# The first feed-forward matrix by seven block products, the second one afterwards from DRAM

## The chip, the cores and the metric

The kernel runs on one core of a Trainium2 chip. The metric is the device time of one execution in microseconds, as the median of several. The profile is that of one further execution; its span is what its trace covers.

## The reference

A trunk of two layers over 1024 tokens of width 1024. Layer 0 mixes tokens by a state-space recurrence, layer 1 by dilated attention; behind each stands the same feed-forward block, of 2816 features. Only that block and its neighbours matter here:

```python
def conv_glu_ffn(x, w_up, conv_w, conv_b, w_down):
    hcat = x @ w_up                       # 1024x1024 by 1024x5632
    hp = jnp.pad(hcat, ((0, 0), (CONV_WIDTH - 1, 0), (0, 0)))
    hcat = conv_b + sum(conv_w[k] * hp[:, CONV_WIDTH - 1 - k:CONV_WIDTH - 1 - k + seq]
                        for k in range(CONV_WIDTH))
    val, gate = jnp.split(hcat, 2, axis=-1)
    return (jax.nn.silu(gate) * val) @ w_down     # 1024x2816 by 2816x1024

h = post_norm(h, mix, ln_gain[layer, 0], ln_bias[layer, 0])
ffn = conv_glu_ffn(h, ffn_w_up[layer], ...)
h = post_norm(h, ffn, ln_gain[layer, 1], ln_bias[layer, 1])
```

post_norm is a layer norm of a weighted sum of h and the block's result. Everything is computed in float32.

## The kernel before

**Products.** A float32 product is done as three matmuls (mm3, L86 to L90): each operand x is split into hi, a rounded copy, and lo = x - hi (split, L81): ACT makes hi (L83), DVE lo (L84). The three are hi by hi, hi by lo, lo by hi. One matmul instruction takes a 128x128 block of weights and 512 columns.

**Order.** Engines run independently, each its own list of instructions in order. That list is fixed when the kernel is built, by a scheduler that follows the program's order and the free buffers of the pools. All loads and stores spoken of here are issued by SP, in SP's order, onto one queue.

**The feed-forward block** (ffn, 22 tiles of 128 features, each a value tile and a gate tile). out_proj leaves eight accumulators of 128 tokens by 1024, normalized without gain and bias; to_T (L160) turns them on PE (32 transposes for each half of the tokens), applies gain and bias and splits them into hT. For each feature tile, `up` loads 512 KB of weights, splits them (wh, wl) and does 2 halves of tokens x 8 x 3 = 48 matmuls into a PSUM tile of 1024 tokens; the causal convolution over three tokens is one ACT instruction (L208) and two DVE instructions (L212) that read PSUM; then silu on ACT (L218), the product on DVE (L219), and a split (ah, al). `down` takes two features at a time (CH = 2): for each of eight token tiles it does 2 x 6 matmuls (L236), and DVE adds the PSUM tile to the accumulator (L242 the first time, L246 after), so up and down alternate through the whole block. ln_affine (L134, L135) puts gain and bias on the eight accumulators by 16 instructions on POOL at the block's start, and `after` (ln_apply in layer 0, ln_final with L141, L145, L146 and L148 in layer 1) ends each token tile. Behind layer 0's block the values of the attention are computed from another to_T.

Pools: xp "x" 16 buffers, rawp 2 (loaded weights), wp 4 (their splits), the block's own "x" 14 and "wd" 4, PSUM "mm" 3 tiles of two banks and "tp" 2 banks.

Of the kernel before, what the change touches and what calls it, by code (L numbers as in the profile page):

```python
# [39 lines left out]
class Net:  # L40
# [119 lines left out]
    def to_T(self, accs, hf, li, xp, tmp):  # L160

        nc = self.nc
        res = []
        for k in range(KT):
            ps = self.psp.tile([P, 512], F32, "tp")
            for q in range(4):
                nc.tensor.transpose(ps[:, q * P : q * P + P], accs[4 * hf + q][:, k * P : k * P + P], self.ident[:])
            x = xp.tile([P, 2, 512], F32R, "x", "hT")
            if k % 2 == 0:
                two = tmp[0].tile([P, 2, 512], F32, tmp[1], "tmp")  # L170
# [1 line left out]
            gain, bias = (self.lnT[:, li, i, k : k + 1] for i in range(2))
            if k % 2:
                nc.vector.tensor_scalar(out=t, in0=ps[:], scalar1=gain, scalar2=bias, op0=ALU.mult, op1=ALU.add)  # L174
            else:
                nc.scalar.activation(t, ps[:], AF.Identity, bias=bias, scale=gain)
# [4 lines left out]

    def ffn(self, l, accs, hT, xp, wd_pool, first_half, after):

        nc = self.nc
# [6 lines left out]
        def start(ft, halves=(0, 1)):
            w = self.wload(a["w_up"][l, ft])
            ps = self.psp.tile([P, T], F32, "mm", "up")
            self.type1(ps, w, hT, halves)
            return w, ps

        def up(f):
            u = []
            for s in range(2):
                ft = f + s * NF  # L200
                if ft in early:
                    w, ps = early[ft]
                    self.type1(ps, w, hT, (1,))
                else:
                    w, ps = start(ft)
                t = xp.tile([P, T], F32, "x", "u")
                tf = t[:]
                nc.scalar.activation(  # L208
                    tf, ps[:], AF.Identity, bias=cw[:, 3, ft : ft + 1], scale=cw[:, 0, ft : ft + 1]
                )  # L210
# [8 lines left out]
            nc.vector.tensor_tensor(out=vf, in0=vf, in1=gf, op=ALU.mult)  # L219
            hi = xp.tile([P, T], F32R, "x", "ah")  # L220
            lo = xp.tile([P, T], F32R, "x", "al")
            self.split(vf, hi[:], lo[:])
            return hi, lo

        def load_down(c, pool, tag):
            return [self.wload(a["w_down"][l, f], pool=pool, tag=tag) for f in c]

        def down(ws, aT, first, last):
            for tt in range(8):
                ps = self.psp.tile([P, D], F32, "mm", "dn")  # L230
                sl = slice(tt * P, tt * P + P)
                for i, (w, x) in enumerate(zip(ws, aT)):
                    ah, al = x[0][:, sl], x[1][:, sl]
# [1227 lines left out]
```

## Time and profile before

| | |
|---|---|
| median of 3 runs | 3149.09 us (3148.43 to 3156.55) |
| profiled execution | 3147.12 us |
| its span | 3145.1 us |
| mean granted clock of TensorE | 0.968 of full speed |
| PE, DVE, ACT, POOL busy | 94%, 51%, 29%, 10% of the span |

The profiled execution takes 2.0 us more than its span and 2.0 us less than the median. Busy is the time in which an engine executes; a matmul's end is modelled, and matmuls overlap, so the rate at which they follow each other is read from counts in a window, not from a mean duration. In a timeline's row the two numbers are the start and the time to the end of a run of like instructions; what stands in brackets is how long the engine had been idle before, and what released it.

### The profile page before, as it was taken

Reading aid. Unit: us, or ns where it says so; the run is one execution under the profiler, and the core shown is the slowest. Engines: PE = TensorE matmul, PEld = TensorE weight load, DVE = VectorE, ACT = ScalarE, POOL = GpSimd, SP = SyncE. Lnnn points to the kernel's source line nnn. Section 1 sums busy time; section 2 is a strip of 40 time slices with the busy share of each in tenths; the row PEclk is TensorE's granted clock in tenths of the full one; section 3 lists DMA queues with packets and bytes.
Section 4 is the critical chain, followed back from the end, with each engine's and each line's share of the span. In section 5 each row is a group of like instructions: output and inputs, shape, how many; then the busy total and the mean of one; then the engine's idle time right before and its main releaser. Section 6 shows DMA issues by size and latency. Waiting matters only on the chain. (4 is left out here: it accounts for less than half of the span.)

```text
span 3145.1 us, 36960 instructions
## 1 busy us (share of the span) xinstructions
PE 2964.7 (94%) x14454; PEld 2456.0 (78%) x14454; DVE 1598.8 (51%) x2773; ACT 922.7 (29%) x1589; POOL 329.7 (10%) x247
## 2 busy tenths in 40 slices
PE   4689999999999999999999999999688999999997
PEld 3668778888888878998777777777567888888886
DVE  8964774544445561113544444344558544544447
ACT  2433332212222231113433344333424322221222
POOL 7920050000000000000000000000253200000001
PEclk8889999999999999999999999999799999999999
DMA  5242421111111143326555456555443111111112
GB/s 176 58 124 63 132 68 53 47 41 47 60 48 47 55 141 101 108 71 163 148 152 150 133 141 151 145 134 137 141 148 102 59 41 54 60 47 41 41 60 74
DMA packets 144926, 295.76 MB, mean 94 GB/s; under 512 B 19057, under 2 KB 60769, under 8 KB 144753
## 3 DMA queue, kind: packets, MB, share of 16 engines
q1 hardware_dynamic: 142640, 283.97, 31.1%
q0 software_dynamic: 2112, 9.44, 0.9%
q8 instruction: 114, 1.87, 0.3%
q14 instruction: 60, 0.48, 0.0%
HBM read 192.08 MB, written 35.20 MB: 72 GB/s over the span
## 5 line engine op out<-in xcount | busy, mean ns | idle before, releaser
L84 DVE TENSOR_TENSOR wl<-raw,wh 128x1024 fp32r<-128x1024 f32 x262 | 336.4, 1291 | 738.7 <-ACT wh L83 737.0
L83 ACT CAST wh<-raw 128x1024 fp32r<-128x1024 f32 x262 | 273.3, 1051 | 1210.5 <-PE up L89 602.3
L89 PE MATMUL up<-hT,wh 128*128 128x512 f32 x1408 | 548.6, 390 | 7.7 <-DVE hT L84 7.7
L90 PE MATMUL up<-hT,wl 128*128 128x512 f32 x1408 | 548.0, 389 | 1.9 <-DVE wl L84 1.9
L88 PE MATMUL up<-hT,wh 128*128 128x512 f32 x1408 | 547.2, 390 | 0.9 <-ACT wh L83 0.9
L88 PE MATMUL qk<-hT,wh 128*128 128x512 f32 x768 | 309.3, 403 | 10.4 <-DVE ql L433 10.4
L89 PEld LDWEIGHTS up<-hT,wh 128*128 128x128 f32 x1408 | 264.3, 188 | 65.6 <-DVE hT L84 11.0
L90 PEld LDWEIGHTS up<-hT,wl 128*128 128x128 f32 x1408 | 264.3, 188 | 57.2 <-DVE wl L84 2.8
L89 PE MATMUL qk<-hT,wh 128*128 128x512 f32 x768 | 308.9, 402 | 0.0
L88 PEld LDWEIGHTS up<-hT,wh 128*128 128x128 f32 x1408 | 264.0, 188 | 56.2 <-ACT wh L83 1.7
L90 PE MATMUL qk<-hT,wl 128*128 128x512 f32 x768 | 307.8, 401 | 0.0
L246 DVE TENSOR_TENSOR acc<-acc,dn 128x1024 f32<-128x1024 f32 x144 | 175.1, 1217 | 117.1 <-PE dn L236 114.8
L212 DVE SCALAR_TENSOR_TENSOR u<-up,cw,u 128x1022 f32<-128x1022 f32 (+1 forms) x176 | 224.6, 1278 | 10.3 <-ACT u L208 8.0
L236 PE MATMUL dn<-wh,ah 128*128 128x512 f32 x704 | 216.9, 389 | 0.0
L236 PE MATMUL dn<-wl,ah 128*128 128x512 f32 x704 | 216.7, 389 | 0.0
L236 PE MATMUL dn<-wh,al 128*128 128x512 f32 x704 | 216.6, 389 | 0.0
L84 POOL TENSOR_TENSOR gT<-oraw,gT 128x512 fp32r<-128x512 f32 x14 | 18.0, 1302 | 1796.2 <-ACT gT L83 1791.8
L88 PEld LDWEIGHTS qk<-hT,wh 128*128 128x128 f32 x768 | 148.3, 193 | 41.8 <-DVE ql L433 12.4
L89 PEld LDWEIGHTS qk<-hT,wh 128*128 128x128 f32 x768 | 148.5, 193 | 29.0
L90 PEld LDWEIGHTS qk<-hT,wl 128*128 128x128 f32 x768 | 148.0, 193 | 29.6
L88 PE MATMUL v<-wh,hT 128*128 128x512 f32 x384 | 152.8, 400 | 1.0 <-DVE tmp L174 1.0
L236 PEld LDWEIGHTS dn<-wl,ah 128*128 128x128 f32 x704 | 132.1, 188 | 27.5
(250 smaller groups left out, 4534.7 us busy)
## 6 DMA issues: line engine op xcount, KB each, us to landing
raw<-in_w_up SPq DMA_DIRECT2D x88, 512.0 KB, 3.5
qs<-qh SPq DMA_DIRECT2D x288, 128.0 KB, 2.4
raw<-in_w_out SPq DMA_DIRECT2D x48, 512.0 KB, 3.5
kl<-ql SPq DMA_DIRECT2D x192, 128.0 KB, 2.4
raw<-in_w_down SPq DMA_DIRECT2D x44, 512.0 KB, 3.5
raw<-in_w_v SPq DMA_DIRECT2D x26, 512.0 KB, 3.7
vscr<-vs SPq DMA_DIRECT2D x48, 256.0 KB, 2.3
V<-vscr SPq DMA_DIRECT2D x24, 512.0 KB, 4.4
```

The lines of the kernel that those rows point to most:

```text
L83: nc.scalar.copy(hi, x)
L84: (eng or nc.vector).tensor_tensor(out=lo, in0=x, in1=hi.bitcast(F32), op=ALU.subtract)
L88: nc.tensor.matmul(out, lh, rh, start=first, stop=False)
L89: nc.tensor.matmul(out, lh, rl, start=False, stop=False)
L90: nc.tensor.matmul(out, ll, rh, start=False, stop=last)
L212: nc.vector.scalar_tensor_tensor(out=tf[:, d:], in0=ps[:, : T - d], scalar=cw[:, d, ft : ft + 1], in1=tf[:, d:], op0=ALU.mult, op1=ALU.add,)
L236: nc.tensor.matmul(ps[:, h * 512 : h * 512 + 512], l_, w[wi][:, h * 512 : h * 512 + 512], start=(i == 0 and l_ is ah and wi == 0), stop=(i ...
L246: nc.vector.tensor_tensor(out=accs[tt][:], in0=accs[tt][:], in1=ps[:], op=ALU.add)
```

## The change

The block is cut into two stages, both over the whole sequence.

**up.** The activations (half 0 and half 1 of the tokens) and the two halves of the 1024 inputs make a 2x2 block matrix; a value tile and a gate tile of weights, each with two halves of the inputs, make the other. Their product, four blocks of 512 tokens by 128 features over two halves of the inputs, is now done by seven block products of 12 matmuls (pa, p2 to p7) instead of eight. For it T1 to T4 (sums and differences of activation blocks, L244 to L253) and B22 are made and split once at the block's start, and s1 to s4 (sums of weight blocks) for each feature; s1, s2, s3, s4 and the gate's second half g2 are split as `piece`, and seven DVE instructions put the products together (L278 to L293), each with one operand in PSUM. The gate's convolution now reads the result in SBUF (L297, L299), its silu follows (L303), and the raw value tile and the finished gate tile are stored to a DRAM tensor `vs` (L294, L304).

**down.** Runs after it, for one half of the tokens at a time: eight PSUM banks hold 4 token tiles by 1024 and sum over all 22 features. The four accumulators are loaded again from `hres`, which out_proj now writes (L1428), with ln_affine on POOL inside this stage. For each feature the value and gate tiles are loaded from `vs` (L352, L353), the 512 KB of w_down are loaded once, kept in SBUF for both halves (L349), and split anew in each half; then the value's convolution (ACT L360, DVE L363 twice), the product (L367), the split (ax), 24 matmuls. The last four features of half 1 are held until their operands are all there, so that the token tiles end one after another. Half 0 of layer 0 is turned for the values inside this stage.

The core of the diff (its other lines move pools and closures):

```diff
-        for i in range(nch):
-            c = list(range(i * CH, i * CH + CH))
-            aT = [up(f) for f in c]
-            if i == nch - 1:
-                ws = load_down(prev[0], wd_pool, "wd") + load_down(c, self.xp, "x")
-                down(ws, prev[1] + aT, first=False, last=True)
-            elif prev:
-                down(load_down(prev[0], wd_pool, "wd"), prev[1], first=(i == 1), last=False)
...
+        for j in range(4):
+            self.turn(accs, 1, 2 * l, j, b12[j], j % 2)
+            tt(out=b0[j], in0=b12[j], in1=b0[j], op=sub)
+            T1.append(part(xp, "x", b0[j]))
+        for j in range(4):
+            self.turn(accs, 1, 2 * l, 4 + j, b22[j], j % 2)
+            B22.append(part(xp, "x", b22[j]))
+            tt(out=b12[j], in0=b22[j], in1=b12[j], op=sub)
+            T3.append(part(fp, "xc", b12[j]))
+            tt(out=b22[j], in0=b0[j], in1=b22[j], op=sub)
+            T2.append(part(fp, "xc", b22[j]))
+            tt(out=b0[4 + j], in0=b0[4 + j], in1=b22[j], op=add)
+            T4.append(part(fp, "xc", b0[4 + j]))
...
+            tt(out=s1, in0=g1, in1=g2, op=add)
+            tt(out=s2, in0=s1, in1=v1, op=add)
+            product(p6[:], piece(s2), T2)
+            tt(out=u2, in0=p6[:], in1=p1, op=add)
+            tt(out=s3, in0=v1, in1=g1, op=add)
+            product(p7[:], piece(s3), T3)
+            tt(out=u3, in0=p7[:], in1=u2, op=add)
+            product(p5[:], piece(s1), T1)
...
+            nc.sync.dma_start(scr[f, :, 0, :], yv[:])
...
+            for t in tts:
+                acc = accp.tile([P, D], F32, "acc", "acc")
+                nc.sync.dma_start(acc[:], hres[t * P : t * P + P, :])
+                self.ln_affine(acc, gb, nc.gpsimd)
...
+            for f in range(NF):
+                if not hf:
+                    W.append(xp.tile([P, D], F32, "x", "wd") if f < 16 else fp.tile([P, D], F32, "xc", "wd"))
+                    nc.sync.dma_start(W[f][:], a["w_down"][l, f])
+                vs = fp.tile([P, 1028], F32, "ws", "vs")
+                nc.sync.dma_start(vs[:, 2 - m : 514], scr[f, :, 0, c0 - m : c0 + 512])
+                nc.sync.dma_start(vs[:, 514:1026], scr[f, :, 1, c0 : c0 + 512])
...
+            nc.sync.dma_start(hres[tt * P : tt * P + P, :], accs[tt][:])
```

How it moves instructions is shown at three places of layer 0. First DVE's list at the block's start, behind the last normalization of out_proj's accumulators (L129). Before, each turned tile (tmp) is split as soon as it is there, and these are the operands of the next matmuls:

```order
L129 TENSOR_SCALAR acc_2894<-acc_2894,mv_3064,r_538_3075 128x1024
L174 TENSOR_SCALAR tmp_3183<-tp_3187,lnT_59 128x512
L84 TENSOR_TENSOR hT_3182<-tmp_3183,hT_3182 128x512
L174 TENSOR_SCALAR tmp_3202<-tp_3206,lnT_59 128x512
L84 TENSOR_TENSOR hT_3192<-tmp_3183,hT_3192 128x512
```

Now (b is a turned tile of half 1, tmp one of half 0, xc a split operand, raw the loaded weights):

```order
L129 TENSOR_SCALAR acc_2904<-acc_2904,mv_3075,r_538_3086 128x1024
L183 TENSOR_SCALAR b_552_3169<-s_3183,lnT_59 128x512
L244 TENSOR_TENSOR tmp_2827<-b_552_3169,tmp_2827 128x512
L183 TENSOR_SCALAR b_553_3170<-s_3203,lnT_59 128x512
L244 TENSOR_TENSOR tmp_2827<-b_552_3169,tmp_2827 128x512
L244 TENSOR_TENSOR tmp_2846<-b_553_3170,tmp_2846 128x512
L183 TENSOR_SCALAR b_554_3171<-s_3234,lnT_59 128x512
L249 TENSOR_TENSOR b_552_3169<-b_554_3171,b_552_3169 128x512
L244 TENSOR_TENSOR tmp_2846<-b_553_3170,tmp_2846 128x512
L183 TENSOR_SCALAR b_555_3172<-s_3276,lnT_59 128x512
L84 TENSOR_TENSOR xc_3180<-tmp_2827,xc_3180 128x512
```

So the turned tiles of all eight blocks come first, sums of them next and splits last. From the second of these rows to the low half of p6's first weight piece DVE has 4 turns and 41 instructions of 512 columns: 16 sums of activation blocks, 20 splits (xc), 4 sums of weights and one piece. PE's list has, ahead of p6, 48 matmuls (the first two value tiles, on half 0) and the 32 transposes; behind them the first matmul that needs a piece's low half is the ninth.

Second, SP's list. Before, the weights of up and down come in turn, as they are used:

```order
L75 DMA raw_3924<-in_w_up 128x1024
L75 DMA raw_3983<-in_w_up 128x1024
L75 DMA raw_4048<-in_w_down 128x1024
L75 DMA raw_4054<-in_w_down 128x1024
L75 DMA raw_4172<-in_w_up 128x1024
```

Now, where up ends and down begins (wd is a kept tile of w_down, the first vs a tile for down, gb gain and bias):

```order
L304 DMA vs_3100<-cv_6125 128x1024
L349 DMA wd_6953<-in_w_down 128x1024
L352 DMA vs_6299<-vs_3100 128x512
L353 DMA vs_6299<-vs_3100 128x512
L349 DMA wd_6994<-in_w_down 128x1024
L349 DMA wd_7035<-in_w_down 128x1024
L349 DMA wd_7076<-in_w_down 128x1024
L349 DMA wd_7117<-in_w_down 128x1024
L352 DMA vs_6340<-vs_3100 128x512
L353 DMA vs_6340<-vs_3100 128x512
L349 DMA wd_6461<-in_w_down 128x1024
```

Between the tiles of feature 0, 1, 2, 3 and 4 that down reads stand 4, 3, 6 and 0 loads of w_down, and behind feature 3's the four accumulators from hres, each 512 KB.

Third, DVE's list at the same place. Before, with up and down alternating, it reads:

```order
L219 TENSOR_TENSOR u_3297<-u_3297,u_3325 128x1024
L84 TENSOR_TENSOR al_3332<-u_3297,ah_3331 128x1024
L84 TENSOR_TENSOR wl_3431<-raw_3428,wh_3430 128x1024
L212 SCALAR_TENSOR_TENSOR u_3359<-up_3152,cw_3082,u_3359 128x1023
L212 SCALAR_TENSOR_TENSOR u_3359<-up_3152,cw_3082,u_3359 128x1022
```

Now, behind the last feature of up, features 0 and 1 of down:

```order
L293 TENSOR_TENSOR yv_6156<-p_1046_6158,yv_6156 128x512
L299 SCALAR_TENSOR_TENSOR cv_6263<-yg_6157,cw_3098,cv_6263 128x1022
L84 TENSOR_TENSOR ax_6306<-cv_6307,ax_6306 128x512
L363 SCALAR_TENSOR_TENSOR cv_6348<-vs_6340,cw_3098,cv_6348 128x511
L363 SCALAR_TENSOR_TENSOR cv_6348<-vs_6340,cw_3098,cv_6348 128x510
L367 TENSOR_TENSOR cv_6348<-cv_6348,vs_6340 128x512
L84 TENSOR_TENSOR ax_6347<-cv_6348,ax_6347 128x512
L84 TENSOR_TENSOR wl_6385<-wd_6379,wh_6384 128x1024
```

The convolution's instructions read two tiles of SBUF where L212 read one of PSUM, and each feature brings five such instructions to DVE (L363 twice, L367, two of L84).

## Rows read from the trace of the kernel before

**Rows 1.** Page, first part: busy time, share of the span, instructions.
```profile
PE 2964.7 (94%) x14454; PEld 2456.0 (78%) x14454; DVE 1598.8 (51%) x2773; ACT 922.7 (29%) x1589; POOL 329.7 (10%) x247
```

**Rows 2.** Windows, both layers' blocks: busy (count) of PE, PEld, DVE, ACT, POOL; clock, DMA.
```profile
500.00:600.00 100.00, 100.00 (x443) 82.81 (x442) 42.92 (x36) 20.81 (x20) 0.00 (x0) 1.00 0.13 42
2600.00:2700.00 100.00, 100.00 (x443) 82.81 (x442) 51.46 (x43) 26.31 (x25) 0.00 (x0) 1.00 0.18 58
```

**Rows 3.** Page, fifth part: PE's groups in the block.
```profile
L89 PE MATMUL up<-hT,wh 128*128 128x512 f32 x1408 | 548.6, 390 | 7.7 <-DVE hT L84 7.7
```

**Rows 4.** Timeline of PE: first and last matmul of both blocks, and eight transposes.
```profile
389.11 0.39 PE L88 MATMUL up<-hT,wh 128*128 128x512 f32 x1
...
1118.02 0.62 PE L236 MATMUL dn<-wh,al 128*128 128x512 f32 x2
1118.48 1.03 PE L167 MATMUL tp<-ident,acc 128*128 128x128 f32 x8
...
2396.27 0.39 PE L88 MATMUL up<-hT,wh 128*128 128x512 f32 x1
...
3125.64 0.61 PE L236 MATMUL dn<-wh,al 128*128 128x512 f32 x2
```

**Rows 5.** Windows, start of layer 0's block.
```profile
400.00:425.00 25.00, 19.23 (x91) 14.06 (x90) 21.48 (x16) 11.87 (x16) 22.57 (x9) 1.00 0.06 19
```

**Rows 6.** Groups of DVE by shape: count, busy us, mean ns, idle before.
```profile
L84 DVE TENSOR_TENSOR wl<-raw,wh 128x1024 fp32r<-128x1024 f32 x262 | 336.4, 1291 | 738.7 <-ACT wh L83 737.0
L212 DVE SCALAR_TENSOR_TENSOR u<-up,cw,u 128x1022 f32<-128x1022 f32 x88 | 112.6, 1279 | 2.3
L433 DVE TENSOR_TENSOR ql<-qk,qh 128x512 fp32r<-128x512 f32 x48 | 33.0, 688 | 38.8 <-ACT qh L432 38.7
L174 DVE TENSOR_SCALAR tmp<-tp,lnT 128x512 f32<-128x512 f32 x24 | 19.4, 806 | 15.3 <-PE tp L167 15.2
L84 DVE TENSOR_TENSOR gT<-gy,gT 128x512 fp32r<-128x512 f32 x16 | 10.4, 689 | 0.7
```

**Rows 7.** Groups of ACT by shape.
```profile
L83 ACT CAST wh<-raw 128x1024 fp32r<-128x1024 f32 x262 | 273.3, 1051 | 1210.5 <-PE up L89 602.3 <-DMA raw<-in_w_down 170.5 <-PE qk L89 160.5
L208 ACT ACTIVATE u<-up,cw 128x1024 f32<-128x1024 f32 x88 | 105.7, 1203 | 9.7 <-PE up L90 9.7
L218 ACT ACTIVATE u<-u 128x1024 f32<-128x1024 f32 x44 | 46.7, 1061 | 137.6 <-DVE u L212 137.6
L83 ACT CAST hT<-tmp 128x512 fp32r<-128x512 f32 x48 | 28.3, 618 | 17.0 <-DVE tmp L174 16.2
```

**Rows 8.** Timeline of DVE, end of out_proj and start of the block, layer 0.
```profile
384.92 1.29 DVE L84 TENSOR_TENSOR hT<-tmp,hT 128x512 fp32r<-128x512 f32 x2
...
396.55 1.53 DVE L129 TENSOR_SCALAR acc<-acc,mv,r 128x1024 f32<-128x1024 f32 x2
400.88 0.81 DVE L174 TENSOR_SCALAR tmp<-tp,lnT 128x512 f32<-128x512 f32 x1 [2.80 <-PE tp L167]
```

**Rows 9.** Windows in out_proj of layer 1.
```profile
2300.00:2305.00 5.00, 5.00 (x23) 4.13 (x22) 2.87 (x1) 0.00 (x0) 5.00 (x2) 1.00 1.03 417
2305.00:2310.00 5.00, 1.75 (x8) 1.13 (x6) 0.00 (x0) 0.00 (x0) 5.00 (x4) 1.00 0.90 355
2310.00:2315.00 5.00, 3.02 (x7) 1.98 (x8) 3.50 (x2) 2.09 (x2) 5.00 (x2) 0.71 0.18 28
```

**Rows 10.** Page, sixth part: loads of w_down.
```profile
raw<-in_w_down SPq DMA_DIRECT2D x44, 512.0 KB, 3.5
```

**Rows 11.** Timeline of POOL and DVE where both work, layer 0 and layer 1.
```profile
400.00 10.80 POOL L134 TENSOR_TENSOR acc<-acc,gb 128x1024 f32<-128x1024 f32 x4 [215.41 <-DMA gb<-in_ln]
403.62 7.73 DVE L84 TENSOR_TENSOR hT<-tmp,hT 128x512 fp32r<-128x512 f32 x3
...
422.31 3.65 DVE L212 SCALAR_TENSOR_TENSOR u<-up,cw,u 128x1023 f32<-128x1023 f32 x3
...
2299.49 3.38 DVE L84 TENSOR_TENSOR wl<-raw,wh 128x1024 fp32r<-128x1024 f32 x1 [2.86 <-ACT wh L83]
```

**Rows 12.** Groups of POOL by shape.
```profile
L134 POOL TENSOR_TENSOR acc<-acc,gb 128x1024 f32<-128x1024 f32 x24 | 66.7, 2805 | 320.4 <-DMA gb<-in_ln 277.4 <-DMA acc<-h 36.8 <-PE tp L167 6.2
```

**Rows 13.** Groups of DVE by shape: layer 1's last normalization.
```profile
L141 DVE SCALAR_TENSOR_TENSOR acc<-acc,mv,gb 128x1024 f32<-128x1024 f32 x8 | 14.2, 1779 | 0.0
```

More of the change, by code (lines that the diff above doesn't have):

```diff
@@ L162, in to_T @@
         nc = self.nc
[L163 removed]
+        res, parts = [], []
         for k in range(KT):
[L165 to L167 removed]
             x = xp.tile([P, 2, 512], F32R, "x", "hT")
             if k % 2 == 0:
[L170 removed]
+                two = tmp.tile([P, 2, 512], F32, "t", "tmp")
@@ L171, in to_T @@
             t = two[:, k % 2, :]
[L172 to L176, printed above, removed]
+            self.turn(accs, hf, li, k, t, k % 2)
             self.split(t, x[:, 0, :], x[:, 1, :])
             res.append(x)
-        return res
-    def ffn(self, l, accs, hT, xp, wd_pool, first_half, after):
+            parts.append(t)
@@ L184, in ffn, with turn @@
+        return res, parts
+    def turn(self, accs, hf, li, k, t, on_vector):
         nc = self.nc
-        CH = 2
-        a = self.a
+        ps = self.psp.tile([P, 512], F32, self.tp)
+        for q in range(4):
+            nc.tensor.transpose(ps[:, q * P : q * P + P], accs[4 * hf + q][:, k * P : k * P + P], self.ident[:])
+        gain, bias = (self.lnT[:, li, i, k : k + 1] for i in range(2))
+        if on_vector:
+            nc.vector.tensor_scalar(out=t, in0=ps[:], scalar1=gain, scalar2=bias, op0=ALU.mult, op1=ALU.add)
+        else:
+            nc.scalar.activation(t, ps[:], AF.Identity, bias=bias, scale=gain)
@@ L187, in ffn @@
+    def ffn(self, l, accs, half0, xp, tm, fp, accp, hres, after):
+        nc, a = self.nc, self.a
         cw = self.cp.tile([P, 4, 2 * NF], F32, "cw")
         nc.sync.dma_start(cw[:], a["convT"][l])
-        early = {}
[L191 to L209, printed above, removed]
-                )
+        scr = self.dp.tile([NF, P, 2, T], F32, name=f"vs{l}")
+        self.up(l, accs, half0, cw, scr, xp, tm, fp, accp)
+        self.down(l, cw, scr, xp, tm, fp, accp, hres, after)
@@ L219, in up @@
[L219 to L233, printed above, removed]
-                    for (l_, wi) in ((ah, 0), (ah, 1), (al, 0)):
-                        for h in range(2):
-                            nc.tensor.matmul(
-                                ps[:, h * 512 : h * 512 + 512], l_, w[wi][:, h * 512 : h * 512 + 512],
-                                start=(i == 0 and l_ is ah and wi == 0),
-                                stop=(i == len(ws) - 1 and l_ is al),
-                            )
-                if first:
-                    nc.vector.scalar_tensor_tensor(
-                        out=accs[tt][:], in0=accs[tt][:], scalar=ALPHA, in1=ps[:], op0=ALU.mult, op1=ALU.add
-                    )
-                else:
-                    nc.vector.tensor_tensor(out=accs[tt][:], in0=accs[tt][:], in1=ps[:], op=ALU.add)
-                if last:
-                    after(tt)
@@ L266 @@
+                self.split(t, x[:, 0], x[:, 1])
+                if late:
+                    kept.append((f, w, x))
+                else:
+                    for i in range(4):
+                        mms(i, f, w, x)
+            for i in range(4):
+                for k in kept:
+                    mms(i, *k)
+                finish(i)
 NG = 3
@@ L1290, in glu, with out_proj @@
     return gT
-def out_proj(net, w, gT, load, accp, middle):
+def out_proj(net, w, gT, load, accp, hres, middle):
     nc = net.nc
```

183 lines of the change are left out of this document (141 added, 42 removed).

## The prediction

> **What bounds the kernel now.** I read the engines' shares first: PE is busy 94%, DVE 51%, ACT 29% [rows 1]. Then windows inside the feed-forward blocks [rows 2]: 443 matmuls in each 100 us, PE busy throughout, at a granted clock of 1.00 (the 2.4 GHz level). So a matmul costs 100/443 = 0.2257 us. The mean of 390 ns in PE's groups [rows 3] overlaps with the next one and is no price. Then where a block begins and ends [rows 4]: 389.1 to 1118.6 in layer 0 and 2396.3 to 3126.3 in layer 1, 729.5 and 730.0 us. A block has 44 x 48 + 22 x 48 = 3168 matmuls, 715.0 us, and 32 transposes, eight of which take 1.03 us [rows 4], 4.1 us. What is left, 10.4 and 10.9 us, is all the idle time of PE, over half of it near the start, where 25 us hold 19.23 us of PE [rows 5]. The block is a chain of matmuls with next to no gaps: a matmul less is worth its 0.2257 us, and a gap that appears costs in full.
>
> **The change part by part.**
>
> *Matmuls removed.* A value and gate pair takes 7 x 12 = 84 matmuls instead of 96; 22 x 12 = 264 less in a layer, 528 x 0.2257 = -119.2 us. Down keeps its 1056.
>
> *Inside up, nothing.* PE needs 84 x 0.2257 = 19.0 us for a feature. DVE does sixteen instructions of 512 columns (4 sums, 5 low halves, 7 combinations, one operand of these in PSUM): 0.69 us each from either kind of row [rows 6], 0.645 back to back [rows 8], so 10.3 to 11.0; a weight split of 1.29 and two convolution steps of 1.28 [rows 6]: 14.2 to 14.9 us. ACT has 1.05 + five casts of 0.62 + a copy (as a cast) 0.62 + 1.20 + 1.06 [rows 7] = 7.0 us. DMA moves four tiles of 512 KB, 2.1 MB in 19 us, 110 GB/s where 417 GB/s were seen [rows 9]. PE covers all three, DVE with 4 us to spare. If that cover goes, each microsecond of a feature costs 44.
>
> *Start of up: +26 a layer.* DVE finishes the last normalization at 396.55 + 1.53 = 398.1, 9.0 us after out_proj's last matmul, and the first turn follows at 400.9 [rows 8], 11.8 us after. Behind it stand four turns at 0.81 (or ACT's share beside them) and 41 instructions before p6 flows: 3.2 + 41 x 0.645 to 0.69 = 29.6 to 31.5 us. So p6 flows 41 to 43 us after PE's first matmul of the block. PE has 48 matmuls (10.8), 32 transposes (4.1) and eight early matmuls (1.8): 16.7 us of work. Idle: 24.7 to 26.6; I take 26. Before, the splits fed matmuls one by one. Bounds: 20, if DVE finds 6 us of the sums to do between the normalization's end and the last transposes; 33, if each of the 21 splits and the piece waits 0.3 us for ACT's cast, which takes 0.62 [rows 7], as long as DVE's half.
>
> *Between up and down: +39 a layer.* Down's first operands wait for two things. One is SP's queue. At the end of up 22 loads of w_down, gain and bias and four accumulators, 28 x 0.52 MB, go through the same queue as the small tiles of vs, as their buffers come free. Landing takes 3.5 us on an idle queue [rows 10]; queued, 0.52 MB at 417 GB/s takes 1.26 us, at 355 GB/s 1.48 [rows 9]. Four, three and six such loads stand ahead of the tiles of features 1, 2 and 3, four accumulators ahead of feature 4's, so these arrive some 6, 11, 20 and 26 us after feature 0's (with their own two tiles, 5, 9, 16 and 21 pieces of 1.26). PE consumes a feature in 24 x 0.2257 = 5.4 us, so feature 0's own latency (about 4 us from the last combination to its first matmul) and gaps of 1.5, 0.5 and 7 us follow: 13 us. The other is POOL. When the accumulators land, 16 ln_affine instructions start, 2.81 us each [rows 12]. Before, where POOL worked, three DVE splits of two SBUF operands took 7.73 us, 2.58 each, instead of 0.69, and a wide one took 3.38; three convolution steps with an operand in PSUM took 3.65, undisturbed [rows 11]. So DVE's instruction with two SBUF operands waits for one POOL instruction each. Down's five per feature are all of that kind: four of 512 at up to 2.81 and one of 1024 at 3.38 = 14.6 us a feature against PE's 5.4. Sixteen POOL instructions make about three features late by 9.2 each, less what was prepared ahead: 26. Together 39. Bounds: 13 (POOL's work finds PE with stock), 48 (the queue at 355 GB/s throughout).
>
> The Trainium skill ("SBUF — State Buffer", section "SBUF: two separate sides") says that VectorE, with two SBUF inputs, and GpSimd share one port pair by an exclusive lock, the loser waiting for the whole instruction. The trace agrees: 2.58 against 0.69 in the rows named. By that rule the convolution, which moves from PSUM to SBUF, loses its immunity; were it no lock but a split of bandwidth, the 26 us above would shrink to a few.
>
> *Inside down, nothing.* A feature costs DVE 1.29 + two steps and a product at 0.69 + a low half 0.69 = 4.1 us, ACT 1.05 + a convolution step (half of 1.20) + 0.62 = 2.3, under PE's 5.4; in a chain of ACT and DVE without overlap about 4.9. With 0.5 us to spare it is thin: a microsecond more would cost 2 x 22 x 2.
>
> *From half 0 to half 1: +9 in layer 0, +13 in layer 1.* Half 1's first matmul wants a bank that DVE empties only after the last matmul of half 0 that fills it. All banks end with the last feature; the four finishes (two instructions of 0.69 each) stand on DVE between statistics and the next features' work, the first at once and the last some 9 us later. In layer 1 the final normalization adds L141, 1.78 us a tile [rows 13], on DVE.
>
> *End of the block.* In layer 0 half 0 is turned early, -4. Layer 1's last tiles end one by one, as before: 0.
>
> *The old idle time goes:* -10.4 - 10.9 = -21.3. *The clock:* after a gap of 3 us PE ran at 0.71 for 5 us [rows 9], 1.5 us lost; two long gaps a layer: +6. *hres stores* in out_proj are not waited for: 0, or +3 if loads queue behind them.
>
> *Sum:* -119.2 + 52 + 78 + 22 - 4 - 21.3 + 6 = +13.5. On the profiled execution's 3147.1 that is 3160.6; the median is 2.0 above that execution, so 3163.
>
> **The rivals.**
>
> *A, the gaps are short and the matmuls win (faster).* At one place, between up and down: w_down's loads are issued while up's last features still compute, so the queue is empty in time, and POOL's 16 instructions fall where DVE has stock. For it: PE's consumption of 19 us a feature leaves the queue at 110 GB/s, and layer 0's POOL work before cost PE under 6 us [rows 5]. Against: buffers for w_down come free only as up's last operands are used. With 15 there instead of 39 and 22 at the start: -119.2 + 44 + 30 + 22 - 4 - 21.3 + 4 = -44.5, 3105. It decides below 30 us a layer.
>
> *B, the queue and the lock add up (slower still).* The accumulators of half 1, too, land while down waits, all of POOL's instructions meet DVE's, and half 1 starts late: 30 at the start, 48 between, 15 at the half: -119.2 + 60 + 96 + 30 - 4 - 21.3 + 8 = +49.5, 3199. For it: the interleaving of SP's list; against: half 1's buffers free slowly.
>
> *C, DVE sets the pace inside up.* If the seven combinations, which wait for a product each, hold back the pieces behind them in DVE's list, a feature takes 20 us instead of 19: +44 on the forecast, 3207. Against: 4 us to spare, pieces one feature ahead.
>
> **How the numbers follow.** Chances: forecast 0.45, A 0.32, B 0.15, C 0.08. The forecast's own range is 3140 to 3185. The range takes in A and B: 3080 to 3205. This kernel's measurement tells 0.3%, 9.4 us, from no change: 3139.6 to 3158.5. A is faster but for a little; of the forecast over a third is within 0.3% and some 0.07 of it below. Faster 0.34, same 0.18, slower 0.48.
>
> **What would show it.** 3696 matmuls of up over both layers, at 0.226 us, 443 to 100 us with PE busy throughout inside up and down; if PE has gaps there, C is right. PE idle some 25 us behind out_proj with DVE busy throughout. Between up and down, PE idle near 39 us with POOL's L134 and L135 at 2.8 us or more beside L363, L367 and L84 at 2.6 or more; short gaps and DVE at 0.69 mean A. If the queue is the cause, vs tiles land late after issue, beside w_down's at over 350 GB/s. A sum of the gaps below 100 us proves the forecast wrong on the faster side.

## The result, and the profile after

The changed kernel takes 3203.76 us (median of 4 runs, 3193.41 to 3206.2) against 3151.2 us of the kernel before in the same comparison (4 runs, 3148.43 to 3156.55): a ratio of 1.0158, interval 1.0132 to 1.0185. It is slower by 1.6%, 41 us above the forecast of 3163: inside the stated range, but only 1.2 us below its upper end of 3205, and outside the forecast's own range of 3140 to 3185. The profiled execution took 3193.41 us with a span of 3191.6, 46.5 more than the span before; it is the fastest of the four, so the accounts below, which go by it, explain 46.5 us and not the whole difference of the medians.

First part of the page after (it answers to [rows 1]): 528 matmuls less, and PE still busy 91%, since the span grew.

```profile
PE 2902.1 (91%) x13926; PEld 2379.3 (75%) x13926; DVE 1958.4 (61%) x3581; ACT 1118.6 (35%) x1965; POOL 327.5 (10%) x247
```

Windows of the kernel after, columns as in [rows 2]. In order: start of layer 0's block, a part of it where PE stands still, inside up (twice), between up and down, a part of that, inside down, the change from half 0 to half 1; then the same places of layer 1.

```profile
388.00:440.00 52.00, 28.52 (x123) 22.26 (x122) 43.07 (x78) 20.33 (x36) 0.00 (x0) 0.77 0.19 65
410.00:420.00 10.00, 0.00 (x0) 0.00 (x0) 10.00 (x18) 2.36 (x6) 0.00 (x0) 0.53 0.00 0
440.00:840.00 400.00, 400.00 (x1725) 323.88 (x1724) 289.44 (x396) 145.00 (x188) 0.00 (x0) 1.00 0.33 115
500.00:600.00 100.00, 100.00 (x432) 81.00 (x431) 72.30 (x99) 36.30 (x47) 0.00 (x0) 1.00 0.31 110
840.00:930.00 90.00, 57.52 (x198) 44.34 (x197) 65.73 (x48) 20.73 (x26) 44.65 (x16) 0.77 0.67 253
870.00:880.00 10.00, 1.83 (x9) 1.18 (x7) 8.00 (x4) 1.77 (x2) 9.51 (x4) 0.74 1.03 406
930.00:1010.00 80.00, 80.00 (x355) 66.23 (x354) 58.51 (x74) 35.83 (x45) 0.00 (x0) 1.00 0.34 99
1010.00:1040.00 30.00, 25.34 (x99) 19.70 (x98) 29.87 (x63) 12.30 (x18) 0.00 (x0) 0.89 0.29 89
2420.00:2470.00 50.00, 26.59 (x116) 20.92 (x116) 41.65 (x76) 19.22 (x34) 0.00 (x0) 0.76 0.19 63
2470.00:2870.00 400.00, 400.00 (x1725) 323.90 (x1724) 290.32 (x397) 146.12 (x189) 0.00 (x0) 1.00 0.32 112
2870.00:2960.00 90.00, 59.82 (x212) 46.04 (x211) 67.49 (x49) 22.59 (x28) 45.66 (x16) 0.81 0.71 270
3040.00:3090.00 50.00, 37.51 (x144) 28.96 (x143) 49.62 (x76) 23.33 (x30) 9.55 (x4) 0.86 0.30 100
```

What a window loses is its length less its matmuls at the 0.2257 us of before (and less 3.65 us for the 32 transposes, which are in the counts of the two starts). Busy time doesn't tell it: from 440 to 840 us PE is busy for all of 400.00 us at full clock, and 1725 matmuls should take 389.3.

| lost by PE, us | layer 0 | layer 1 | forecast, clock included |
|---|---|---|---|
| start of the block | 52 - 91 x 0.2257 - 3.65 = 27.8 | 50 - 84 x 0.2257 - 3.65 = 27.4 | 27.5 |
| inside up | 400 - 1725 x 0.2257 = 10.7 | 10.7 | 0 |
| between up and down | 90 - 198 x 0.2257 = 45.3 | 90 - 212 x 0.2257 = 42.2 | 40.5 |
| half 0 to half 1 | 30 - 99 x 0.2257 = 7.7 | 50 - 144 x 0.2257 = 17.5 | 9 and 13 |

A loss has two parts. PE's idle time is the window less PE's busy time: 23.5 and 23.4 us at the start, 32.5 and 30.2 between up and down, 4.7 and 12.5 at the half, 127 in all. The other 41 us of these three rows (4.3 and 4.0, 12.8 and 12.0, 3.0 and 5.0) are busy time: matmuls that take longer than 0.2257 us, in windows whose granted clock is 0.76 to 0.89 on the mean.

Timeline of PE (it answers to [rows 4]): out_proj's last matmul, the 32 transposes, matmuls that waited at the borders of layer 0, and the last of down in layer 1.

```profile
388.25 0.39 PE L90 MATMUL wo<-wh,gT 128*128 128x512 f32 x1
391.14 0.47 PE L88 MATMUL pa<-hT,wh 128*128 128x512 f32 x1 [2.49 <-DVE acc L1424]
...
402.13 3.65 PE L180 MATMUL s<-ident,acc 128*128 128x128 f32 x32
425.54 0.79 PE L88 MATMUL p<-xc,wc 128*128 128x512 f32 x1 [19.76 <-ACT wc L83]
...
852.39 1.22 PE L332 MATMUL dn<-wh,ax 128*128 128x512 f32 x2 [3.49 <-ACT ax L83]
...
882.88 1.22 PE L332 MATMUL dn<-wh,ax 128*128 128x512 f32 x2 [11.05 <-ACT ax L83]
...
908.47 1.22 PE L332 MATMUL dn<-wh,ax 128*128 128x512 f32 x2 [7.04 <-ACT ax L83]
...
924.09 1.22 PE L332 MATMUL dn<-wh,ax 128*128 128x512 f32 x2 [8.07 <-ACT ax L83]
...
1148.18 0.76 PE L88 MATMUL v<-wh,hT 128*128 128x512 f32 x1 [2.43 <-DVE acc L340]
...
3179.19 0.63 PE L332 MATMUL dn<-wh,ax 128*128 128x512 f32 x2
```

Two waits were not foreseen, 2.49 at the start and 2.43 at the end: each time PE wants the banks of a stage that follows, and DVE is still emptying the last tile of the one before. The first is part of the loss at the start, the second ends layer 0's block. Behind a long gap PE starts again at the lower level of its clock (1.2 GHz): two matmuls take 1.22 us, where 0.63 is usual.

Between up and down, the rows that the forecast asked for: DVE's L363, L367 and L84 before and beside POOL's L134 and L135, in layer 0 (they answer to [rows 11]).

```profile
862.20 1.53 DVE L363 SCALAR_TENSOR_TENSOR cv<-vs,cw,cv 128x511 f32<-128x511 f32 x2
...
870.49 5.65 POOL L134 TENSOR_TENSOR acc<-acc,gb 128x1024 f32<-128x1024 f32 x2 [686.16 <-DMA acc<-hres]
876.10 2.78 POOL L135 TENSOR_TENSOR acc<-acc,gb 128x1024 f32<-128x1024 f32 x1
...
873.87 5.56 DVE L363 SCALAR_TENSOR_TENSOR cv<-vs,cw,cv 128x511 f32<-128x511 f32 x2
879.47 2.71 DVE L367 TENSOR_TENSOR cv<-cv,vs 128x512 f32<-128x512 f32 x1
...
896.01 3.40 DVE L84 TENSOR_TENSOR wl<-wd,wh 128x1024 fp32r<-128x1024 f32 x1
```

Two steps take 1.53 alone and 5.56 beside POOL, 2.78 each, the length of one POOL instruction. And the loads issued from 830 to 935 us, with the median time from issue to landing, which was 3.5 for w_down's before [rows 10]:

```profile
wd<-in_w_down SPq DMA_DIRECT2D x22, 512.0 KB, 9.0
vs<-vs SPq DMA_DIRECT2D x28, 256.0 KB, 7.7
acc<-hres SPq DMA_DIRECT2D x8, 512.0 KB, 9.0
```

### The profile page after: what moved, and what is told of

It reads as the page before. It is cut to its first block, busy times and chain, and to the rows that moved or that the text cites. A ratio compares the mean times of both kernels' runs of the same rounds, so it can differ in the third digit from the quotient of the medians.

```text
span 3191.6 us, 38175 instructions
## 1 busy us (share of the span) xinstructions
PE 2902.1 (91%) x13926; PEld 2379.3 (75%) x13926; DVE 1958.4 (61%) x3581; ACT 1118.6 (35%) x1965; POOL 327.5 (10%) x247
## 4 chain that ended last, share of the span: by engine, by line
PE 78%; DVE 9%; POOL 4%; DMA 4%; issue 2%; ACT 1%; SPq 1%; DVEq 0%; POOLq 0%; ACTq 0%
PE dn L332 13%; PE p L90 8%; PE p L88 7%; PE p L89 7%; PE qk L88 6%; PE qk L90 6%; PE qk L89 6%; PE o L745 3%; PE v L88 3%; PE v L90 3%; PE v L89 3%; PE t L735 2%; PE s L608 2%; DVE cv L363 1%; PE pa L88 1%
## 5 line engine op out<-in xcount | busy, mean ns | idle before, releaser
L332 PE MATMUL dn<-wh,ax 128*128 128x512 f32 x1408 | 400.5, 404 | 79.8 <-ACT ax L83 77.8
L88 PE MATMUL p<-xc,wc 128*128 128x512 f32 x880 | 351.7, 400 | 40.9 <-ACT wc L83 21.1
L84 DVE TENSOR_TENSOR wl<-raw,wh 128x1024 fp32r<-128x1024 f32 x174 | 221.8, 1276 | 272.1 <-ACT wh L83 268.9
L332 PEld LDWEIGHTS dn<-wh,ax 128*128 128x128 f32 x1408 | 273.0, 195 | 147.0 <-ACT ax L83 85.3
L89 PE MATMUL p<-xc,wc 128*128 128x512 f32 x880 | 350.6, 398 | 0.0
L90 PE MATMUL p<-xc,wc 128*128 128x512 f32 x880 | 348.8, 398 | 1.1 <-DVE wc L84 1.1
L332 PE MATMUL dn<-wl,ax 128*128 128x512 f32 x704 | 231.3, 410 | 0.0
L88 PEld LDWEIGHTS p<-xc,wc 128*128 128x128 f32 x880 | 167.2, 190 | 82.3 <-ACT wc L83 22.8
L83 ACT CAST wc<-s 128x512 fp32r<-128x512 f32 x176 | 108.2, 621 | 268.4 <-PE p L90 242.9
L89 PEld LDWEIGHTS p<-xc,wc 128*128 128x128 f32 x880 | 167.6, 190 | 40.5
L90 PEld LDWEIGHTS p<-xc,wc 128*128 128x128 f32 x880 | 166.1, 189 | 42.5 <-DVE wc L84 2.5
L134 POOL TENSOR_TENSOR acc<-acc,gb 128x1024 f32<-128x1024 f32 x24 | 67.3, 2823 | 1265.3 <-DMA acc<-hres 692.4
L88 PEld LDWEIGHTS qk<-hT,wh 128*128 128x128 f32 x768 | 147.9, 193 | 41.7 <-DVE ql L546 12.4
L90 PEld LDWEIGHTS qk<-hT,wl 128*128 128x128 f32 x768 | 147.6, 192 | 29.6
L363 DVE SCALAR_TENSOR_TENSOR cv<-vs,cw,cv 128x512 f32<-128x512 f32 (+2 forms) x176 | 160.3, 912 | 8.7 <-ACT cv L360 5.9
L332 PEld LDWEIGHTS dn<-wl,ax 128*128 128x128 f32 x704 | 141.3, 201 | 31.7
L596 DVE CUSTOM_DVE_ANT_0 p<-s,bt 128x256 f32<-128x256 f32 (+1 forms) x384 | 119.0, 370 | 66.2 <-PE s L608 65.6
```

The costliest lines, as they stand in the source:

```text
L83: nc.scalar.copy(hi, x)
L84: (eng or nc.vector).tensor_tensor(out=lo, in0=x, in1=hi.bitcast(F32), op=ALU.subtract)
L88: nc.tensor.matmul(out, lh, rh, start=first, stop=False)
L89: nc.tensor.matmul(out, lh, rl, start=False, stop=False)
L90: nc.tensor.matmul(out, ll, rh, start=False, stop=last)
L134: eng.tensor_tensor(out=acc[:], in0=acc[:], in1=gb[0][:], op=ALU.mult)
```

## The experiments

The base is the changed kernel; each edit is a difference to it. A ratio is against the kernel before. Stage times are differences of starts in PE's timeline: start = last matmul of out_proj to first piece product, up = first to last piece product, gap = from there to down's first matmul, down = its first to last matmul. They are those of one profiled execution each, and such executions differ by some us where no edit reaches: from the last matmul of layer 0's down to out_proj's last in layer 1 the changed kernel takes 1274.4 us, the others 1277.9 to 1288.8.

| us, layer 0 / 1 | start | up | gap | down |
|---|---|---|---|---|
| changed kernel | 37.3 / 37.2 | 423.0 / 422.7 | 3.9 / 4.2 | 292.7 / 295.3 |
| e1, no ln_affine in down | 38.8 / 39.4 | 423.2 / 422.9 | 4.2 / 3.3 | 268.7 / 275.4 |
| e5, ln_affine on DVE | 39.7 / 38.9 | 422.9 / 423.1 | 5.0 / 3.5 | 271.8 / 279.9 |
| e9, e1 with half of w_down's loads | 38.8 / 40.8 | 423.3 / 422.8 | 2.4 / 3.7 | 260.0 / 264.2 |
| e4, w_down from ACT | 37.3 / 39.2 | 422.7 / 423.1 | 21.1 / 23.9 | 281.8 / 290.0 |
| e6, e5 with w_down from POOL | 38.8 / 40.3 | 423.2 / 423.2 | 5.3 / 4.9 | 272.0 / 277.7 |
| e8, turns first | 36.4 / 39.2 | 409.5 / 409.9 | 3.8 / 3.7 | 293.0 / 296.0 |
| e3, four early value tiles | 50.7 / 50.7 | 412.9 / 412.9 | 4.7 / 4.2 | 290.7 / 294.8 |
| e2, width 1056 | 37.2 / 39.7 | 418.4 / 418.3 | 3.7 / 3.8 | 291.2 / 294.3 |
| e7, width 1152, 4 buffers | 38.9 / 39.6 | 413.4 / 413.2 | 9.5 / 9.5 | 287.9 / 292.2 |
| e10, width 1088 | 38.8 / 39.3 | 412.8 / 413.3 | 4.4 / 4.1 | 290.7 / 294.3 |
| f1, e5 + e8, width 1024 | 38.1 / 38.9 | 398.8 / 400.5 | 5.7 / 3.6 | 286.9 / 288.9 |
| f2, e5 + e8 + e10 | 38.0 / 40.0 | 399.8 / 399.3 | 4.7 / 3.8 | 271.6 / 273.3 |

**Is it POOL that delays down? (e1, e5).** e1 drops ln_affine from down; e5 has it on DVE.

```diff
-                self.ln_affine(acc, gb, nc.gpsimd)      # e1: line removed
+                self.ln_affine(acc, gb, nc.vector)      # e5: this in its place
```

> Leaves out gain and bias of the residual in down (16 POOL instructions a layer); everything else as in the changed kernel (3204 us). Theory, lock: DVE's instructions on two SBUF tiles wait for POOL's; without POOL, L363, L367 and L84 take 0.69 between up and down, and of the 45 us that PE loses there in a layer some 26 to 30 go: 3144 to 3152 us. Rival, queue: the tiles of vs arrive late whatever POOL does, so the gaps stay within 5 us a layer: 3194 to 3204.

> The 16 ln_affine instructions of down go from POOL to DVE, nothing else; the result is whole. Theory, lock: on DVE they cost 1.2 us each, 19 us a layer, most of it in time in which DVE waits for PE or for loads, so first to last matmul of down takes 270 to 278 us instead of 293 to 295 (269 and 275 without them) and the whole 3165 to 3175. Rival, DVE's own load: the 19 us fall where DVE is late anyway and replace what the lock cost: 285 us or more, 3190 to 3204.

e1: 3162.93 us, ratio 1.0023 (1.0011 to 1.0034); e5: 3164.29, ratio 1.0034 (1.0021 to 1.0046). Down falls by 24.0 and 19.9 us in e1, by 20.9 and 15.4 in e5, and the whole by 40.8 and 39.5. e1 gives less than the 26 to 30 a layer that were expected, but far more than its rival's 5; e5 came out close to its theory. The group of the first convolution step, in the changed kernel and then in e1 (a line earlier there):

```profile
L363 DVE SCALAR_TENSOR_TENSOR cv<-vs,cw,cv 128x511 f32<-128x511 f32 x44 | 47.6, 1081 | 6.0 <-ACT cv L360 5.9
```
```profile
L362 DVE SCALAR_TENSOR_TENSOR cv<-vs,cw,cv 128x511 f32<-128x511 f32 x44 | 32.9, 747 | 6.8 <-ACT cv L359 6.7
```

Without POOL's work the mean is 747 ns, with it 1081. The medians of e5 and e1 differ by 1.4 us only, which their intervals don't separate (in the profiled executions e5's down is 3.1 and 4.5 us longer): DVE has the time for the work, so it is the meeting of the two engines that was dear. What remains of PE's gaps in e1 (848 to 910 us), at features 0, 3 and 6 of down, is next:

```profile
857.42 1.22 PE L331 MATMUL dn<-wh,ax 128*128 128x512 f32 x2 [3.75 <-ACT ax L83]
...
881.02 1.22 PE L331 MATMUL dn<-wh,ax 128*128 128x512 f32 x2 [4.20 <-ACT ax L83]
...
904.65 1.22 PE L331 MATMUL dn<-wh,ax 128*128 128x512 f32 x2 [4.21 <-ACT ax L83]
```

**Is the rest the order of SP's queue, or the bandwidth? (e4, e6, e9).** e4 takes w_down's loads to ACT's queue, e6 to POOL's (on e5). e9 (on e1) loads the first 11 tiles of w_down only and uses them twice.

```diff
-                    nc.sync.dma_start(W[f][:], a["w_down"][l, f])
+                    nc.scalar.dma_start(W[f][:], a["w_down"][l, f])     # e4
+                    nc.gpsimd.dma_start(W[f][:], a["w_down"][l, f])     # e6
...
-                if not hf:
+                if not hf and f >= 11:                                  # e9
+                    W.append(W[f - 11])
+                elif not hf:
```

> The 22 loads of w_down are issued by ACT on its own queue instead of SP's. Theory, queue order: the tiles of vs for features 1 to 3 no longer stand behind w_down, the first gaps (13 us in a layer) shrink by about 8: 3188. Rival, shared bandwidth or a waiting ACT: the loads still take the same 28 us of transfer and ACT waits for free buffers at the end of up, 3200 to 3215.

> As e5_affine_dve, and the 22 loads of w_down are issued by POOL, which has nothing else to do there, instead of SP. Theory, queue order: the tiles of vs are no longer behind w_down, three gaps of about 4 us in a layer and the slow clock behind them go, another 8 to 12 us a layer: 3145 to 3157. Rival, bandwidth: 14 MB have to pass before and beside the first features whichever queue they stand in, gaps move but stay: 3162 to 3180.

> As e1_no_affine (no ln_affine in down), and only the first 11 tiles of w_down are loaded and used twice, so 5.8 MB a layer less pass between up and down (it leaves out half of w_down). Theory, bandwidth: what is left of the gaps between up and down without POOL (three of about 4 us and the slow clock behind them) comes from loads that share 400 GB/s; first to last matmul of down falls from 269 and 275 us to 258 and 264, the whole to 3140. Rival, latency of the chain load, ACT, DVE, PE: the gaps stay, 3160.

e4: 3230.69 us, ratio 1.023 (1.0207 to 1.0252), 27 us slower than the change and worse than either expectation: ACT, which has work of its own, now waits with these loads. Down itself is 10.9 and 5.3 us shorter, but the gap ahead of it is 17.2 and 19.7 longer. Down's first matmul in PE's timeline, and among the waits (total, times, longest) ACT's for these loads:

```profile
870.13 1.22 PE L332 MATMUL dn<-wh,ax 128*128 128x512 f32 x2 [20.72 <-ACT ax L83]
```
```profile
ACT wh L83 <- DMA wd<-in_w_down: 44.5, 4, 21.7
```

e6: 3177.81 us, ratio 1.0064 (1.0043 to 1.0085), as its rival has it, with the same length of down as e5: the small tiles no longer stand behind the large ones in one queue, and PE still waits. The loads of 830 to 935 us in e5, then in e6, show why: on a queue of their own vs's tiles land hardly sooner, and w_down's much later.

```profile
wd<-in_w_down SPq DMA_DIRECT2D x22, 512.0 KB, 9.0
vs<-vs SPq DMA_DIRECT2D x32, 256.0 KB, 7.4
```
```profile
wd<-in_w_down POOLq DMA_DIRECT2D x22, 512.0 KB, 16.1
vs<-vs SPq DMA_DIRECT2D x34, 256.0 KB, 6.4
```

e9: 3142.26 us, ratio 0.9965 (0.9952 to 0.9978), 21 us below e1. PE's gaps in the same stretch of e9:

```profile
854.02 0.93 PE L331 MATMUL dn<-wh,ax 128*128 128x512 f32 x2 [1.98 <-ACT ax L83]
...
862.16 0.73 PE L331 MATMUL dn<-wh,ax 128*128 128x512 f32 x2 [0.80 <-ACT ax L83]
```

So what is left beside POOL is the amount of data that has to land at once: half of w_down is worth 8.7 and 11.2 us of down. e9 alone would fit the order in the queue too, since it also halves what stands ahead of the small tiles; it is e6 that shows the order not to decide. e6's median is 14 us above e5's, but their profiled executions have equal blocks (out_proj's last matmul to down's last: 739.6 and 739.6 us in layer 0, 745.8 and 746.3 in layer 1), and the intervals of the two ratios touch (1.0021 to 1.0046, 1.0043 to 1.0085); where a difference would come from is not shown.

**Is PE's gap at the start due to too little filler, or to late turns? (e3, e8).** e3 gives PE four value tiles ahead of the pieces; e8 puts the transposes of half 1 behind the first value tile, and three more value tiles behind them.

```diff
-        for f in range(2):
+        for f in range(4):        # e3
...
+        start(0)                  # e8: first value tile
+        split[1] = values(1)
...
+        for j in range(4):
+            self.turn(accs, 1, 2 * l, 4 + j, b22[j], j % 2)
+        for f in range(1, 4):
+            start(f)              # e8: three more, behind the turns
```

> Four instead of two value tiles are multiplied by the half-0 operands before the sums are ready. Theory, start: PE is idle there only for want of operands; 48 more matmuls lie in the gap, 10.8 us a layer, so 3182. Rival, PSUM: four held banks leave too few for the seven products, PE waits for them behind the gap instead: 3195 to 3210.

> The 32 transposes of half 1 come on PE behind the first value tile instead of the second, and the products of three more value tiles behind them. Theory, start: DVE's chain of turns, sums and splits (30 us) starts 4 to 5 us earlier, and 48 more matmuls (10.8 us) lie beside it, so from out_proj's last matmul to the first product of a sum 36 to 38 us pass as before but with 48 more matmuls done in it, up is 10.8 us shorter: 3175 to 3183. Rival: the splits of the two further weight tiles (1.2 us each on DVE) and waits for PSUM eat it, 3195 or more.

e3: 3207.32 us, ratio 1.016 (1.014 to 1.0179), no gain: up has 10 us less to do, and the start is 13.5 longer. The time is in its rival's range, but not for the rival's reason: PE's long wait is for the first piece, as before, and not for PSUM. The transposes stand behind the extra products in PE's list, so DVE's chain begins later and the gap moves whole. e8: 3183.27 us, ratio 1.0089 (1.007 to 1.0108), 20 us better. First piece product in e3, then in e8:

```profile
441.95 0.80 PE L88 MATMUL p<-xc,wc 128*128 128x512 f32 x1 [19.54 <-ACT wc L83]
```
```profile
425.21 0.80 PE L88 MATMUL p<-xc,wc 128*128 128x512 f32 x1 [6.04 <-ACT wc L83]
```

The length of DVE's chain is the price of the start, as forecast, and e8 leaves it as it was (36.4 and 39.2 us); it lays 48 more matmuls beside it, so that PE waits 13.7 us less at this place. Up is 13.5 and 12.8 us shorter, a little more than the 10.8 of these matmuls: in the 10 us behind the wait the granted clock is 0.70 instead of 0.55.

**Why does a piece product take longer? (e2, e7, e10).** Inside up five of seven products read their weights from tiles of the pool "ws". From start to start in PE's timeline, 500 to 800 us, a matmul of these takes 0.2335 us on the mean, one of the two others 0.2288, and one of the kernel before 0.2267. (A window also counts the matmul that crosses its edge, so the 0.2257 from its count is 0.4% low.) The tiles are 1028 columns wide; the edits change only that (e7 has four of the wider buffers in place of five).

```diff
-                t = fp.tile([P, 1028], F32R, "ws", "wc")
+                t = fp.tile([P, 1056], F32R, "ws", "wc")     # e2; 1152 in e7, 1088 in e10
...
-                vs = fp.tile([P, 1028], F32, "ws", "vs")
+                vs = fp.tile([P, 1056], F32, "ws", "vs")     # likewise, and tmp's four
```

> Tiles that hold the weight pieces are 1056 instead of 1028 columns wide, so that all five start at the same offset in a row of 128 bytes as the split weights that PE reads at 0.226 us a matmul. Theory, address: the pieces' products step at 0.2333 because of where their stationary operand lies; the step goes to 0.226 and 2 x 22 x 60 matmuls give back 19 us: 3185. Rival, something else in these products (the moving operand, what runs beside them): the step stays 0.233, 3204.

> Tiles of the weight pieces are 1152 columns wide and there are four instead of five, so that all start at the same offset in a row of 512 bytes as the other operands of PE. Theory, address: with a width of 1056 the first and the fifth tile, 512 bytes apart in phase, stepped at 0.2275 us and the three between at 0.2325; now all step at 0.2265 to 0.2275, up takes 411 to 414 us a layer instead of 423, the whole 3182 to 3185. Rival, something in the middle products: they stay at 0.2325, up 418. Four tiles instead of five may cost a wait a feature; then PE shows gaps.

> The changed kernel with one number changed, the width of the tiles of the weight pieces: 1088 columns instead of 1028; five tiles, everything else as it was. Theory, address: all five products step at 0.2267, up takes 413 us a layer instead of 423 and nothing else moves: 3204 - 20 = 3184. Rival: the width alone gives a part of it, as 1056 did (4.5 us a layer, 3192), and the rest of what f2_width_1088 showed came with its other two edits.

e2: 3192.52 us, ratio 1.0114 (1.0094 to 1.0134), half of what was looked for. e7: 3193.3, ratio 1.0121 (1.0105 to 1.0137): up falls by 9.6 and 9.5 us, and a part is lost again in the gap, 9.5 for 4, with one buffer less. e10: 3184.79, ratio 1.0101 (1.0082 to 1.012), up shorter by 10.2 and 9.4. Windows of e2 and of e10 inside up:

```profile
500.00:600.00 100.00, 100.00 (x437) 81.91 (x437) 72.29 (x98) 37.02 (x48) 0.00 (x0) 1.00 0.29 107
```
```profile
500.00:600.00 100.00, 100.00 (x443) 82.81 (x442) 73.97 (x101) 37.25 (x48) 0.00 (x0) 1.00 0.31 111
```

432, 437 and 443 matmuls at widths of 1028, 1056 and 1088, in one and the same order of instructions: the width alone does it, and 443 is the count of before [rows 2]. In e10 a matmul of either kind takes 0.2267 us.

**All together (f1, f2).** f1 is e5 and e8 with tiles of 1024 columns, where the gate's half of `vs` goes to the free half of another buffer ("cv"). f2 is e5, e8 and the width of 1088.

```diff
+                cv = tm.tile([P, D], F32, "t", "cv")                          # f1
+                t, gate = cv[:, :512], cv[:, 512:]
-                nc.sync.dma_start(vs[:, 514:1026], scr[f, :, 1, c0 : c0 + 512])
+                nc.sync.dma_start(gate, scr[f, :, 1, c0 : c0 + 512])
```

> The three repairs together on the changed kernel: ln_affine of down on DVE, the transposes of half 1 first with three more early value tiles, and all tiles of weight pieces 4096 bytes apart (1024 columns; down's gate tile goes into the unused half of the convolution's tile). If each saves what it saved alone (40, 21 and, for all five products at 0.2267, 20 us), the whole takes 3204 - 81 = 3123 us, 1% under the kernel before. Rival: they overlap, since each filled idle time of DVE that another one needs: 3140 to 3155, not clearly faster.

> As f1_all_three, but the tiles of the weight pieces are 1088 columns wide (4352 bytes apart) and hold the gate tile as before. Theory, address: the first, third and fifth tile have the phase of 512 bytes of the other operands, the second and fourth do not; three products of five step at 0.227 to 0.228, two at 0.2325, up takes 4 us a layer longer than in f1_all_three. Rival, the gate's new place decides more than the address: f1_all_three is late in down by more than it wins in up.

f1: 3154.74 us, ratio 1.0006 (0.9997 to 1.0014), some 30 us worse than expected and in its rival's range, though not because the gains overlap, as f2 shows. f2: 3124.76 us (3117.11 to 3129.58), ratio 0.9908 (0.9892 to 0.9924): faster than both kernels. The two have the same up; down differs by 15.3 and 15.6 us. The longest wait at the start of down in f1 (its second feature) and in f2 (its fourth):

```profile
864.70 1.22 PE L340 MATMUL dn<-wh,ax 128*128 128x512 f32 x2 [18.79 <-ACT ax L83]
```
```profile
865.24 1.22 PE L340 MATMUL dn<-wh,ax 128*128 128x512 f32 x2 [5.21 <-ACT ax L83]
```

Where the gate is put is the one thing besides the width that sets them apart, and up shows that the width is as good in either. In f1's list of DVE eight instructions of ln_affine stand between the second feature's convolution and its product (L376), and the first of them waits for its accumulator. In f2 the product (L375) has none ahead of it. DVE in f1, then in f2:

```profile
854.10 1.23 DVE L134 TENSOR_TENSOR acc<-acc,gb 128x1024 f32<-128x1024 f32 x1 [6.87 <-DMA acc<-hres]
...
863.31 0.68 DVE L376 TENSOR_TENSOR cv<-cv 128x512 f32<-128x512 f32 x1
```
```profile
846.02 0.69 DVE L375 TENSOR_TENSOR cv<-cv,vs 128x512 f32<-128x512 f32 x1
```

That the gate's load, waiting for a buffer of the convolution, is what put these instructions ahead is inferred, not shown. f2's time agrees with the sum of its parts: 3203.76 less 39.5 (e5), 20.5 (e8) and 19.0 (e10) is 3124.8. That it agrees to a tenth is chance, as runs of one kernel spread by 10 us. The expectation that some of f2's products would stay slow was a miss: its window from 450 to 820 us has 1634 matmuls, as in e10, where the changed kernel has 1596.

## Why the prediction was right, and where it was off

- **Direction and range** were right, the range by 1.2 us. What carries the direction was right too: the matmuls saved are as many as forecast (13926 left), and the waits at four borders of stages give them back. The size was not: two costs were put at next to nothing, "inside up" and the clock, and the waits were put too high, which hid a part of it.
- **Start of up** came out as forecast, 27.8 and 27.4 against 27.5, in part by chance. DVE is busy throughout where PE stands still (410 to 420 us). But of the 26 us of idle time 23.5 came, and 2.5 of these are the wait for PSUM, which the forecast lacked; the slow clock behind it costs 4.3 and 4.0 instead of 1.5. DVE's chain takes 27.7 us from the first turn (403.20) to the first matmul that uses a piece's low half (430.91), where 29.6 to 31.5 were worked out: behind each other its instructions of 512 columns step at 0.60 us, not 0.645 to 0.69.
- **"Inside up, nothing" is the step that failed.** It is mis-sized at 0 where 10.7 us a layer were measured. DVE, ACT and DMA were covered as the step says (DVE busy 72%, no gap on PE), but its other premise, that a piece product costs what any matmul costs, did not hold: 0.2335 us against 0.2267 at a width of 1028. e10 gives 19 us back by the width alone. Rival C had a cost of this kind, per feature and inside up, and with 3207 the nearest time, but for another reason, which the rows exclude: PE never waits there.
- **The clock** was put at +6 for both layers, from one gap in out_proj. At the start, between up and down and at the half the windows show 41 us. Down has not one long gap but several in a row, and PE starts each time anew at the lower level.
- **Between up and down** the place and the lock were right: 45.3 and 42.2 lost against 40.5. But PE's idle time in it was too high in the forecast, 39 against 32.5 and 30.2, and the clock too low, 1.5 against 12.8 and 12.0. The lock was put at 26 us a layer; e1 measures 24.0 and 19.9, the clock behind its waits included. The Trainium skill ("SBUF — State Buffer", section "SBUF: two separate sides") calls it an exclusive lock for the whole instruction, and the trace agrees: 2.78 beside an instruction of 2.78. The queue was put at 13 us, in the first four features; without POOL, e1 has waits of 3.75 + 4.20 + 4.21 = 12.2 in layer 0, at features 0, 3 and 6. But the prediction explained it by the order in SP's list, and e6 refutes that as the cause: another queue leaves the wait where it was.
- **Half change:** 7.7 and 17.5 against 9 and 13. The bank that half 1's first matmul wants costs PE 0.20 us in either layer; its long waits there (4.16 in layer 0, 7.88 in layer 1) are for a later feature's operands, which stand behind the normalization in DVE's list. In layer 1 four POOL instructions fall into it (9.55 us in the window's row). They are not ln_affine but L146 of the final normalization, which the forecast left out, and they stand there in e1 too (9.52 us). The lock is met again: DVE's instructions of one column with two operands in SBUF (L121, L124) take 2.03 to 2.44 us beside them, where such a one took 0.15 just before; one with a single operand between them (L122) takes 0.15. Rows of DVE, and POOL's:

```profile
3065.08 0.15 DVE L124 TENSOR_TENSOR r<-r,t 128x1 f32<-128x1 f32 x1
...
3066.60 2.40 DVE L124 TENSOR_TENSOR r<-r,t 128x1 f32<-128x1 f32 x1
...
3071.39 0.15 DVE L122 TENSOR_SCALAR t<-t 128x1 f32<-128x1 f32 x1
...
3066.49 7.17 POOL L146 TENSOR_TENSOR acc<-acc,gb 128x1024 f32<-128x1024 f32 x3 [116.28 <-ACT acc L145]
```

- **The rivals.** What B says of the accumulators happened: all eight land between up and down, and all 16 POOL instructions fall there (x8 and x16 in the rows). But its 48 of idle time between and 15 at each half are too high, and its time of 3199 holds nothing for up: it is near by chance. Rival A's gaps of 15 us did not come.
- **End of the block:** put at 0. Layer 0 has the wait of 2.43. In layer 1 the last matmul stands 3191.6 - 3179.19 = 12.4 us before the span's end, where it was 3145.1 - 3125.64 = 19.5: 7.1 gained, not forecast.
- **Turning early:** from the first value matmul of layer 1 to out_proj's last there are 2396.04 - 1120.60 = 1275.4 us before and 2419.8 - 1148.18 = 1271.6 after: -3.8 against -4. That is not clear of the spread of this stretch over the runs. And it moves work more than it saves any: all 32 transposes of half 0 now stand in down.

The sum on the profiled executions: -119.2 + 55.2 (start) + 21.4 (up) + 87.5 (between) + 25.2 (halves) + 2.4 - 21.3 (old idle) - 3.8 - 7.1 = +40.3, of 46.5 measured. Of the other 6, 1.5 are the transposes of half 0: 32 of them (3.65 us) in layer 0's down, where twelve (2.1 us) stood between down and the first value matmul before. The rest is spread and was not traced. The profiled difference exceeds the forecast of 13.5 by 33 us: up adds 21.4 and the clock 35, and the idle time at the borders, 127 instead of 152, takes 25 off, together 31 of them.

## What to carry to other kernels

A saving of matmuls is paid for at the borders of the stages that it creates: count there the chain that feeds the first product, the burst of loads, the engines that hinder each other, and the slower clock behind long waits, and put the transposes that feed a chain ahead of the filler work that is to cover it. Work for GpSimd that was cheap beside VectorE instructions with an operand in PSUM becomes dear when these read two SBUF tiles; try it on VectorE, if that engine has time. Don't take a matmul's price over to operands in new tiles, and compare counts per 100 us, since a busy share of 100% at full clock hid a loss of 2.5%.
